# Stick-breaking attention on one core: scores and value products of four heads each in one run of matmuls

## The chip, the cores and the metric

The kernel runs on one core of a Trainium2 chip. The metric is the device time of one execution in microseconds (us), as the median of several runs. The engines are named as in the profile: PE is TensorE's matmul, PEld its weight load, DVE VectorE, ACT ScalarE, POOL GpSimd, SP the engine that issues most DMAs.

## The reference

A trunk of two layers on 256 tokens of 1024 features, in float32. Each layer has a mixer, cross attention into 256 memory tokens, and a squared-ReLU MLP. The mixer of the second (odd) layer is stick-breaking attention with 16 heads of 64 features:

```python
def _odd_mixer(h, w_in, w_out):
    s = h.shape[1]
    pos = jnp.arange(s)
    q, k, v = jnp.split(h @ w_in, 3, axis=-1)
    ...
        strict = pos[None, :] < t[:, None]
        z = jnp.einsum('bhqd,bhkd->bhqk', qb, k).astype(jnp.float32) * SB_SCALE
        log_beta = jax.nn.log_sigmoid(z)
        log_keep = jnp.where(strict, jax.nn.log_sigmoid(-z), 0.0)
        between = lax.cumsum(log_keep, axis=3, reverse=True) - log_keep
        a = jnp.where(strict, jnp.exp(log_beta + between), 0.0)
        return jnp.einsum('bhqk,bhkd->bhqd', a.astype(v.dtype), v)
    ...
    return _merge(o) @ w_out
```

So a key's weight is the sigmoid of its score times the product of sigmoid(-z) over all later keys that the query may see.

## The kernel before

The residual stream stays on chip, transposed: features on partitions, 256 tokens on the free axis. The weights stream through SBUF once, as units of [128, 1024] float32 (512 KB). SP loads a unit into one of four `raw` buffers; ACT casts it in two halves of 512 columns to a rounded part (`wh`, line 144), and DVE subtracts to get the remainder (`wl`, line 145); four units of each can stand ready. A projection takes three passes (high by high, high by low, low by high), so one unit is 24 matmuls of 256 columns (line 154). In the odd mixer the projections of a group's queries and keys are two units each; the values, with tokens on partitions, take two units that are both read by each token tile.

`mixer1` (lines 517 to 571) goes over four groups of four heads. For a group it projects q, k and v, and multiplies the queries and keys by the reciprocal norms on DVE (lines 528 and 531); ACT copies the values out of PSUM with theirs (`evac_nat`, line 253). Then it takes the group's heads in two pairs, `pp`. A head of a pair, `hh`, lies on 64 of the 128 partitions, so its score matmul uses 64 rows of the array (line 540):

```python
                for tt, (a, b, s) in enumerate(((0, 128, 128), (128, 384, 256))):
                    for hh in range(2):
                        rs = slice(64 * hh, 64 * hh + 64)
                        nc.tensor.matmul(ps[hh][:, a:b], lhsT=q[rs, pp, tt * P:(tt + 1) * P],
                                         rhs=k[rs, pp, 0:s], start=True, stop=True)
```

A head's scores are 384 columns: 128 keys for the first 128 queries, 256 keys for the second. These products are float32, and each is two records in the trace, one for each of two passes. For each head DVE adds the mask to the two diagonal blocks (548), ACT takes Sigmoid of -z (`keep`, 550) and of z (`beta`, 551), DVE scans `keep` backwards (552) and multiplies `beta` by the shifted scan in two pieces (555), and POOL sets the last column of each piece to zero (557). PE then transposes three blocks a head (`transposes`, line 309), ACT copies them out (311), and the value products follow (564), which write 64 partitions each, so they use 64 columns of the array. A pair's output is split into a rounded part and a remainder (165, 166).

After the fourth group come three parts of the cross attention's keys and values (`fill(1, 3)`) and the output projection. PE executes strictly in the order of the program, and that order is made by a scheduler from the program's dependencies and its own estimates: it moves the attention's matmuls of one group among the projections of the next, unless `keep_in_program_order` ties an instruction to the one that stands before it in the source.

PSUM has eight banks of 512 float32 columns: three `mm` for projections, two `sc`, and one each `tr`, `po`, `sm`. The scores use `sc`, the transposes `tr`, the value products `po`; `sm` is used for norms.

Of the kernel before, what the change touches and what calls it, by code (L numbers as in the profile page):

```python
"""Two-layer hybrid encoder trunk on one core.

The residual stream stays on chip, transposed: features on partitions, the 256 tokens on the free
axis.  Weights stream through SBUF once, in pieces of [128, 1024].  A float32 product of a weight
and an activation is taken as three float32r passes over an exact split of each operand into a
rounded part and its remainder (hi*hi + hi*lo + lo*hi).  The reciprocal norms of an RMSNorm are
applied to the products' results; its gains are applied to the activations before.
"""
# [9 lines left out]
F32 = mybir.dt.float32  # L18
F32R = mybir.dt.float32r
AF = mybir.ActivationFunctionType  # L20
# [3 lines left out]
P = 128  # L24
# [8 lines left out]
# columns of the constant table  # L33
# [6 lines left out]
C_END = 2688  # L40

# columns of the gain table
# [5 lines left out]
class Split:  # L48
    """Two float32r tiles, [128, 8, 256], that sum to a float32 activation."""
# [6 lines left out]
class Norm(Split):  # L56
    """An RMSNorm of a transposed stream whose reciprocal norm is applied later."""
# [6 lines left out]
    def part(self, src, kt):  # L64
        """Take feature tile kt, [128, 256], of the stream."""
# [25 lines left out]
class Builder:  # L91
# [26 lines left out]
    def ps(self, tag):  # L118
        """One bank of PSUM, from the banks of one kind of use."""
        return self.psum.tile([P, 512], F32, name="ps_" + tag, tag=tag, bufs=self.banks[tag])  # L120
# [4 lines left out]
    def unit(self, name, i, width=1024):  # L125
        """Load weight piece i of an array and split it into a rounded part and its remainder."""
        return self.unit_split(self.unit_load(name, i, width), 2)
# [21 lines left out]
    def passes(self, out, pairs, start=True, stop=True, pin=False, **kw):  # L149
        """out += sum of lhsT * rhs over float32 operands given as (hi, lo) pairs."""  # L150
# [12 lines left out]
    def split_into(self, hi, lo, src):  # L163
        """Exact split of src (SBUF or PSUM) into two float32r parts."""
        self.nc.scalar.copy(out=hi, in_=src)
        self.nc.vector.tensor_tensor(out=lo, in0=src, in1=hi.bitcast(F32), op=ALU.subtract)  # L166
# [6 lines left out]
    def rsqrt_split(self, acc, nat=True, out=None):  # L173
        """rsqrt_mean of one [128, 256] sum over D features, its sum taken in two float32r passes."""
# [10 lines left out]
    def rsqrt_mean(self, accs, n, w=T, nat=True, out=None):  # L185
        """1/sqrt(mean over partitions and tiles + eps) of summed squares, [128, w] on all
        partitions; with nat, columns 256, 257 hold it for both token tiles, tokens on partitions."""
# [6 lines left out]
    def rsqrt_of(self, ps, n, w=T, nat=False, out=None):  # L194
# [13 lines left out]
        # one Newton step: y * (1.5 - 0.5 * ms * y * y)  # L208
# [16 lines left out]
    def proj_t(self, units, n, ps, i):  # L225
        """n-tile i of ps (transposed result) from one [8 kt, 128] weight piece."""
# [10 lines left out]
    def proj_nat(self, name, i, n):  # L237
        """[tokens, 256 columns] for both token tiles, from two [4 kt, 256] pieces."""
# [17 lines left out]
    def out_proj(self, name, o, nxt):  # L256
        """Output projection into the residual stream; feeds the next norm tile by tile."""
# [25 lines left out]
    def fill(self, l, count):  # L283
        """Do up to count of the eight parts of layer l's keys and values."""
# [16 lines left out]
    def transposes(self, p2):  # L301
        """Probabilities of two heads, [t, (tile 0 | tile 1)], to [s, ...] with s on partitions:
        columns 0:256 keys 0..127 for all queries, 256:384 keys 128..255 for queries 128..255."""
# [15 lines left out]
    def softmax_rows(self, ps, tabs, scale, normalise):  # L319
        """exp(scale * (scores + table) - max) of two score tiles, each [t, 128 | 256]."""  # L320
# [27 lines left out]
    def scores(self, parts):  # L348
        """One head's causal scores, [t, 128 | 256]; parts: (q, k) with features on partitions."""
# [9 lines left out]
    def rope(self, dst, x, w):  # L359
        """x*cos + swap(x)*sin over w groups of 256 tokens; dst(rows) gives the place of 64 rows."""  # L360
# [12 lines left out]
    def mixer0(self, n, nxt, first):  # L373
        nc = self.nc
        # latent projections
# [40 lines left out]
        # keys and values of the latent attention  # L416
# [18 lines left out]
        # queries of the latent attention  # L435
# [83 lines left out]
    def mixer1(self, n, nxt):  # L519
# [3 lines left out]
        for g in range(4):  # L523
# [11 lines left out]
            for pp in range(2):  # L535
                ps = [self.ps("sc") for _ in range(2)]
                for tt, (a, b, s) in enumerate(((0, 128, 128), (128, 384, 256))):
                    for hh in range(2):
                        rs = slice(64 * hh, 64 * hh + 64)
                        nc.tensor.matmul(ps[hh][:, a:b], lhsT=q[rs, pp, tt * P:(tt + 1) * P],  # L540
                                         rhs=k[rs, pp, 0:s], start=True, stop=True)
                beta = self.k4.tile([P, 2, 384], F32, name="beta", tag="k4")
                keep = self.k4.tile([P, 2, 384], F32, name="keep", tag="k4")
                sfx = self.k4.tile([P, 2, 384], F32, name="sfx", tag="k4")
                for hh in range(2):
                    z, bt, kp, c = ps[hh][:, 0:384], beta[:, hh, :], keep[:, hh, :], sfx[:, hh, :]
                    diag = z.rearrange("p (b c) -> p b c", b=3)[:, 0::2, :]
# [444 lines left out]
```

## Time and profile before

| | |
|---|---|
| median of 3 runs | 830.42 us (830.34 to 831.72) |
| the profiled execution, first to last instruction | 829.1 us |
| PE busy | 814.9 us, 98% |
| DVE busy | 578.3 us, 70% |
| ACT busy | 448.8 us, 54% |
| mean granted clock of TensorE | 0.992 |
| DMA, mean over the span | 167 GB/s |

The span is that of the profiled execution; its whole time is not given beside it, and the runs' median is 1.3 us above its span, which is what lies around the first and the last instruction. A row of the timeline gives the start and the busy time of an instruction, or of several alike that follow each other (x8). Busy times of neighbours overlap, as PE and DVE are pipelined: what an instruction costs its engine is the step from its start to the next one's.

### The profile page before, as it was taken

The numbers are of one execution on the slowest core, as the hardware profiler recorded it, in microseconds if no ns is written. First come the engines' busy times: TensorE is split into PE (matmuls) and PEld (weight loads), VectorE is DVE, ScalarE is ACT, GpSimd is POOL, SyncE is SP. The second block draws the span as 40 slices with busy tenths as digits, with TensorE's granted clock in tenths as the row PEclk, the third lists the DMA queues.
The fourth block names the chain that finished last, engine by engine and source line by source line (L and its number), as shares of the span: only waits on it lengthen the run. The fifth ranks groups of instructions, "written<-read, shape, count | busy, mean of one in ns | idle before, by whom it ended". The sixth has DMA issues, their size and how long they took to land. (4 is left out here: it accounts for less than half of the span.)

```text
span 829.1 us, 15928 instructions
## 1 busy us (share of the span) xinstructions
PE 814.9 (98%) x6304; PEld 777.9 (94%) x6304; DVE 578.3 (70%) x1066; ACT 448.8 (54%) x924; POOL 60.8 (7%) x100
## 2 busy tenths in 40 slices
PE   8999999999999999999999999999999999999996
PEld 6989999999999999999988888899999999999995
DVE  7799865878686665566678565767759756666565
ACT  5667655756564444444466454565647544444443
POOL 6003000200020000000030000011003000000002
PEclk8999999999999999999999999999999999999998
DMA  8646245753356555555534433355436555555541
GB/s 306 208 133 204 92 162 182 225 181 107 122 186 204 196 180 178 184 186 190 180 129 153 151 120 112 130 175 167 144 97 208 183 195 183 177 187 192 179 152 51
DMA packets 38955, 138.62 MB, mean 167 GB/s; under 512 B 4449, under 2 KB 4705, under 8 KB 38753
## 3 DMA queue, kind: packets, MB, share of 16 engines
q1 hardware_dynamic: 38736, 137.35, 50.2%
q8 instruction: 49, 0.80, 0.4%
q10 hardware_dynamic: 144, 0.26, 0.1%
q14 instruction: 26, 0.20, 0.1%
HBM read 136.55 MB, written 1.05 MB: 166 GB/s over the span
## 5 line engine op out<-in xcount | busy, mean ns | idle before, releaser
L144 ACT CAST wh<-raw 128x512 fp32r<-128x512 f32 (+1 forms) x502 | 285.3, 618 | 273.3 <-issue 135.0
L145 DVE TENSOR_TENSOR wl<-raw,wh 128x512 fp32r<-128x512 f32 (+1 forms) x502 | 331.1, 699 | 142.4 <-ACT wh L144 141.4
L154 PE MATMUL ps_mm<-act_lo,wh 128*128 128x256 f32 x1248 | 356.8, 286 | 1.3 <-DVE act_lo L69 1.2
L154 PE MATMUL ps_mm<-act_hi,wl 128*128 128x256 f32 x1248 | 356.4, 286 | 1.5 <-DVE wl L145 1.5
L154 PE MATMUL ps_mm<-act_hi,wh 128*128 128x256 f32 x1248 | 354.3, 286 | 1.8 <-ACT wh L144 1.1
L154 PEld LDWEIGHTS ps_mm<-act_hi,wl 128*128 128x128 f32 x1248 | 240.2, 192 | 5.2 <-issue 3.0
L154 PEld LDWEIGHTS ps_mm<-act_hi,wh 128*128 128x128 f32 x1248 | 239.3, 192 | 5.2 <-issue 2.3
L154 PEld LDWEIGHTS ps_mm<-act_lo,wh 128*128 128x128 f32 x1248 | 240.0, 192 | 3.9 <-DVE act_lo L69 1.9
L83 POOL TENSOR_TENSOR sq<-sq 128x256 f32<-128x256 f32 x42 | 38.1, 908 | 480.7 <-ACT sq L79 479.6
L154 PE MATMUL ps_mm<-wh,act_hi 128*128 128x256 f32 x224 | 64.9, 290 | 0.0
L154 PE MATMUL ps_mm<-wl,act_hi 128*128 128x256 f32 x224 | 64.2, 287 | 0.6 <-DVE wl L145 0.6
L154 PE MATMUL ps_mm<-wh,act_lo 128*128 128x256 f32 x224 | 63.9, 285 | 0.0
L154 PEld LDWEIGHTS ps_mm<-wh,act_hi 128*128 128x128 f32 x224 | 42.8, 191 | 2.1 <-issue 1.7
L154 PEld LDWEIGHTS ps_mm<-wl,act_hi 128*128 128x128 f32 x224 | 42.8, 191 | 1.3 <-DVE wl L145 0.8
L154 PEld LDWEIGHTS ps_mm<-wh,act_lo 128*128 128x128 f32 x224 | 42.8, 191 | 1.2 <-issue 1.2
L628 DVE SCALAR_TENSOR_TENSOR m<-ps_mm,r 128x512 f32<-128x512 f32 x32 | 22.1, 690 | 27.8 <-PE ps_mm L154 27.8
L154 PE MATMUL ps_sc<-fl,wh 128*128 128x256 f32 x128 | 36.1, 283 | 0.0
L154 PE MATMUL ps_sc<-fh,wl 128*128 128x256 f32 x128 | 36.1, 283 | 0.0
L154 PE MATMUL ps_sc<-fh,wh 128*128 128x256 f32 x128 | 35.9, 283 | 0.0
L69 DVE SCALAR_TENSOR_TENSOR act_lo<-hT,gains,act_hi 128x256 fp32r<-128x256 f32 x48 | 32.4, 695 | 2.6 <-ACT act_hi L68 2.6
L68 ACT ACTIVATE act_hi<-hT,gains 128x256 fp32r<-128x256 f32 x48 | 23.6, 504 | 10.9 <-DVE hT L263 6.3
L154 PE MATMUL ps_sc<-wh,fh 128*128 128x512 f32 x64 | 25.3, 395 | 0.0
(229 smaller groups left out, 1136.8 us busy)
## 6 DMA issues: line engine op xcount, KB each, us to landing
raw<-in_w SPq DMA_DIRECT2D x128, 512.0 KB, 3.4
raw<-in_w_in SPq DMA_DIRECT2D x38, 512.0 KB, 3.4
raw<-in_xkv SPq DMA_DIRECT2D x32, 512.0 KB, 3.5
raw<-in_w_out SPq DMA_DIRECT2D x16, 512.0 KB, 3.3
raw<-in_wq SPq DMA_DIRECT2D x16, 512.0 KB, 3.9
raw<-in_wo SPq DMA_DIRECT2D x16, 512.0 KB, 3.3
raw<-in_memT SPq DMA_DIRECT2D x4, 512.0 KB, 3.8
cst<-in_cst SPq DMA_DIRECT2D x1, 1152.0 KB, 9.2
```

The source lines that it names most:

```text
L68: nc.scalar.activation(out=self.hi[:, kt, :], in_=src, func=AF.Copy, scale=g)
L69: nc.vector.scalar_tensor_tensor(out=self.lo[:, kt, :], in0=src, scalar=g, in1=self.hi[:, kt, :].bitcast(F32), op0=ALU.mult, op1=ALU.subtract)
L83: nc.gpsimd.tensor_tensor(out=self.acc, in0=self.acc, in1=sq, op=ALU.add)
L144: nc.scalar.copy(out=wh[:, s], in_=raw[:, s])
L145: nc.vector.tensor_tensor(out=wl[:, s], in0=raw[:, s], in1=wh[:, s].bitcast(F32), op=ALU.subtract)
L154: ins = self.nc.tensor.matmul(*args, **kws)
L628: nc.vector.scalar_tensor_tensor(out=m, in0=ps, scalar=0.0, in1=self.bc2(r), op0=ALU.max, op1=ALU.mult)
```

## The change

The work of the four heads of a group is gathered in a new function, `stick`. Its eight score matmuls are written one after the other, and all but the first are tied to the one before it (`pinned`). They go to four banks: for each head of a pair, `main` (an `sc` bank, all 512 columns: the first pair's second query tile in 0:256, the second pair's first tile in 256:384, the first pair's first tile in 384:512) and `rest` (`tr` or `sm`, the second pair's second tile). The elementwise operations then take 512 or 256 columns instead of 384, and the product with the scan is one piece. The transposes alternate between the banks `tr` and `sm`. The eight value products are written in one run as well and write the whole `po` bank, and the output is split in one piece of 512 columns. The constant table gets 128 more columns, a scan row of 512 instead of 384. In the last group, the first key and value parts behind the mixer are tied to stand after the scores (`issue_after`).

```diff
-C_END = 2688
+C_END = 2816
...
+    def pinned(self, *args, **kw):
+        self.tc.keep_in_program_order(self.nc.tensor.matmul(*args, **kw))
+
+    def stick(self, g, q, k, v, o):
...
+        main = [self.ps("sc") for _ in range(2)]
+        rest = [self.ps("tr"), self.ps("sm")]
+        first = True
+        for pp, tt, ps, a in ((1, 1, rest, 0), (0, 1, main, 0), (1, 0, main, 256), (0, 0, main, 384)):
+            for hh in (1, 0):
+                rs = slice(64 * hh, 64 * hh + 64)
+                w = P * (tt + 1)
+                (nc.tensor.matmul if first else self.pinned)(
+                    ps[hh][:, a:a + w], lhsT=q[rs, pp, tt * P:(tt + 1) * P], rhs=k[rs, pp, 0:w],
+                    start=True, stop=True)
+                first = False
+        scored = self.tc.nc.cur_bb.bb.instructions[-1]
+        probs = []
+        for ps, w, nd, pool, tag in ((main, 512, 3, self.k4, "k4"), (rest, 256, 1, self.k2, "k2")):
...
+            for hh in range(2):
+                z = ps[hh][:, 0:w]
+                diag = z[:, P:w].rearrange("p (b c) -> p b c", b=nd)
+                nc.vector.tensor_tensor(out=diag, in0=diag, op=ALU.add,
+                                        in1=self.sb_mask[:, None, :].broadcast_to([P, nd, P]))
+                nc.scalar.activation(out=keep[:, hh, :], in_=z, func=AF.Sigmoid, scale=-0.125)
+                nc.scalar.activation(out=beta[:, hh, :], in_=z, func=AF.Sigmoid, scale=0.125)
+                last = beta[:, hh, P:w].rearrange("p (b c) -> p b c", b=nd)[:, :, P - 1:P]
+                nc.gpsimd.memset(last, 0.0)
+                z, c = beta[:, hh, :], sfx[:, hh, :]
+                nc.vector.tensor_tensor_scan(out=c[:, ::-1], data0=keep[:, hh, ::-1],
+                                             data1=self.scan1[:, (512 - w):], initial=1.0,
+                                             op0=ALU.mult, op1=ALU.add)
+                nc.vector.tensor_tensor(out=z[:, 0:w - 1], in0=z[:, 0:w - 1], in1=c[:, 1:w],
+                                        op=ALU.mult)
+            probs.append(beta)
...
+        for pp in range(2):
+            t = self.k4.tile([P, 2, 384], F32, name="pT", tag="k4")
+            pT.append(t)
+            for hh in range(2):
+                ps = self.ps(("tr", "sm")[hh])
+                for b, (src, a) in enumerate(places[pp]):
+                    nc.tensor.transpose(out=ps[:, b * P:(b + 1) * P], in_=src[:, hh, a:a + P],
+                                        identity=self.ident)
+                nc.scalar.copy(out=t[:, hh, :], in_=ps[:, 0:384])
+        po = self.ps2("po")
+        first = True
+        for pp in (1, 0):
+            for blk, (a, b, t0) in enumerate(((0, 256, 0), (256, 384, 128))):
+                for hh in range(2):
+                    rs = slice(64 * hh, 64 * hh + 64)
+                    cs = slice((2 * pp + hh) * 64, (2 * pp + hh) * 64 + 64)
+                    (nc.tensor.matmul if first else self.pinned)(
+                        po[rs, pp, t0:T], lhsT=v[:, blk, cs], rhs=pT[pp][:, hh, a:b],
+                        start=blk == 0, stop=blk == 1)
+                    first = False
+        self.split_into(o.hi[:, 2 * g:2 * g + 2, :], o.lo[:, 2 * g:2 * g + 2, :], po)
+        return scored
...
     def mixer1(self, n, nxt):
...
-            for pp in range(2):
...
-                kt = 2 * g + pp
-                self.split_into(o.hi[:, kt, :], o.lo[:, kt, :], po)
+            scored = self.stick(g, q, k, v, o)
         self.tc.keep_in_program_order(
             nc.scalar.preload_act_table_set("natural_log_exp_and_others"))
-        self.fill(1, 3)
+        with self.tc.issue_after(scored):
+            self.fill(1, 3)
...
-        self.sb_mask, self.scan1 = col(C_SB, P), col(C_SCAN, 384)
+        self.sb_mask = col(C_SB, P)
+        self.scan1 = col(C_SCAN, 512)
...
-    last = np.zeros(384, np.float32)
-    last[[127, 383]] = 1.0
-    c[:, C_SCAN:C_SCAN + 384] = last[::-1]
+    last = np.zeros(512, np.float32)
+    last[[255, 383, 511]] = 1.0
+    c[:, C_SCAN:C_SCAN + 512] = last[::-1]
```

Where the instructions stand. A row gives the line, the operation, what is written and read, the tile's shape, and how many like it follow each other; `ps_mm<-act_hi,wh` is a projection matmul. PE before, group 1's scores, which stand among the query projections of group 2:

```order
L154 MATMUL ps_mm<-wh,act_lo 128x256
L540 MATMUL ps_sc<-sq_k,sq_q 128x128 x2
L540 MATMUL ps_sc<-sq_k,sq_q 128x256 x2
L154 MATMUL ps_mm<-act_hi,wh 128x256
...
L540 MATMUL ps_sc<-sq_k,sq_q 128x128
L540 MATMUL ps_sc<-sq_k,sq_q 128x256
L154 MATMUL ps_mm<-act_hi,wh 128x256
L154 MATMUL ps_mm<-act_lo,wh 128x256
L540 MATMUL ps_sc<-sq_k,sq_q 128x128
L540 MATMUL ps_sc<-sq_k,sq_q 128x256
L154 MATMUL ps_mm<-act_hi,wl 128x256
```

The first pair stands in one run; between it and the second pair's first head are 33 projection matmuls, and between that pair's heads two. In group 0 transposes stand between the two products of the last head as well. PE now, the same place:

```order
L154 MATMUL ps_mm<-wh,act_lo 128x256
L536 MATMUL ps_sm<-sq_k,sq_q 128x256
L520 MATMUL ps_tr<-sq_k,sq_q 128x256
L520 MATMUL ps_sc<-sq_k,sq_q 128x256 x2
L520 MATMUL ps_sc<-sq_k,sq_q 128x128 x4
L154 MATMUL ps_mm<-act_hi,wh 128x256
...
L571 MATMUL ps_sm<-cst,beta 128x128 x3
L154 MATMUL ps_mm<-act_hi,wl 128x256
...
L571 MATMUL ps_tr<-cst,beta 128x128 x3
```

All eight score matmuls stand together in every group, and 59 projection matmuls later come the first transposes. The value products, which before stood as one and three for each pair, are eight in a row in groups 1 to 3; in group 0 the first is alone, four projection matmuls ahead of the other seven. DVE now, behind group 1's scores:

```order
L549 TENSOR_TENSOR ps_sm<-ps_sm,cst 128x128
L549 TENSOR_TENSOR ps_tr<-ps_tr,cst 128x128
L145 TENSOR_TENSOR wl<-raw,wh 128x512 x2
L556 SCALAR_TENSOR_TENSOR sfx<-keep,cst 128x256
L549 TENSOR_TENSOR ps_sc<-ps_sc,cst 128x384
L556 SCALAR_TENSOR_TENSOR sfx<-keep,cst 128x256
L549 TENSOR_TENSOR ps_sc<-ps_sc,cst 128x384
L559 TENSOR_TENSOR beta<-beta,sfx 128x255 x2
L556 SCALAR_TENSOR_TENSOR sfx<-keep,cst 128x512 x2
L559 TENSOR_TENSOR beta<-beta,sfx 128x511 x2
L145 TENSOR_TENSOR wl<-raw,wh 128x512 x2
```

Before, two heads' operations stood between two weight splits; now those of all four heads do (the scan is printed as SCALAR_TENSOR_TENSOR). In group 0 a weight split stands behind each of the first two adds, and the query product of the next group ahead of the two wide products.

## Rows read from the trace of the kernel before

**Rows 1.** The page, part 1: busy time, share of the span and instructions of each engine.
```profile
PE 814.9 (98%) x6304; PEld 777.9 (94%) x6304; DVE 578.3 (70%) x1066; ACT 448.8 (54%) x924; POOL 60.8 (7%) x100
```

**Rows 2.** Busy times by stretches of the odd mixer (number of instructions), granted clock, DMA share, GB/s.
```profile
441.50:466.90 25.40, 25.40 (x190) 21.66 (x188) 16.63 (x33) 14.58 (x29) 0.54 (x8) 1.00 0.38 125
```

**Rows 3.** Who waited for whom, 441 to 545 us: us in total, times, longest.
```profile
DVE wl L145 <- ACT wh L144: 19.0, 10, 4.2
...
PEld ps_mm L154 <- issue: 7.7, 24, 0.4
```

**Rows 4.** PE's timeline, group 0, first score run: start, us, engine, line, what.
```profile
442.29 0.28 PE L154 MATMUL ps_mm<-act_lo,wh 128*128 128x256 f32 x1
442.50 0.93 PE L540 MATMUL ps_sc<-sq_k,sq_q 64*128 64x128 f32 x8
443.35 0.38 PE L154 MATMUL ps_mm<-act_hi,wl 128*128 128x256 f32 x1
443.58 0.28 PE L154 MATMUL ps_mm<-act_hi,wh 128*128 128x256 f32 x1
```

**Rows 5.** PE's timeline, group 1: one head of the second pair.
```profile
471.68 0.28 PE L154 MATMUL ps_mm<-act_lo,wh 128*128 128x256 f32 x1
471.80 0.28 PE L154 MATMUL ps_mm<-act_hi,wl 128*128 128x256 f32 x1
472.01 0.92 PE L540 MATMUL ps_sc<-sq_k,sq_q 64*128 64x128 f32 x4
...
473.08 0.28 PE L154 MATMUL ps_mm<-act_lo,wh 128*128 128x256 f32 x1
```

**Rows 6.** PE's timeline, group 0: the other head of the second pair, split by transposes.
```profile
448.53 0.49 PE L540 MATMUL ps_sc<-sq_k,sq_q 64*128 64x128 f32 x2
448.94 0.44 PE L309 MATMUL ps_tr<-cst,beta 128*128 128x128 f32 x2
449.31 0.70 PE L540 MATMUL ps_sc<-sq_k,sq_q 64*128 64x256 f32 x2
449.94 0.39 PE L154 MATMUL ps_mm<-act_lo,wh 128*128 128x256 f32 x1
```

**Rows 7.** PE's timeline, group 0: transposes and the first value product of a pair.
```profile
452.54 0.49 PE L309 MATMUL ps_tr<-cst,beta 128*128 128x128 f32 x3
452.96 0.65 PE L564 MATMUL ps_po<-pT,sq_v 128*64 128x256 f32 x2
...
453.76 0.28 PE L154 MATMUL ps_mm<-act_hi,wl 128*128 128x256 f32 x1
```

**Rows 8.** PE's timeline, group 0: the other three value products of its second pair.
```profile
463.91 0.28 PE L154 MATMUL ps_mm<-wl,act_hi 128*128 128x256 f32 x1
464.12 0.86 PE L564 MATMUL ps_po<-pT,sq_v 128*64 128x256 f32 x6
...
465.13 0.28 PE L154 MATMUL ps_mm<-wh,act_hi 128*128 128x256 f32 x1
```

**Rows 9.** DVE's timeline, group 1, behind its first score run.
```profile
467.97 0.76 DVE L548 TENSOR_TENSOR ps_sc<-ps_sc,cst 128x256 f32<-128x256 f32 x2 [0.29 <-PE ps_sc L540]
468.64 1.28 DVE L145 TENSOR_TENSOR wl<-raw,wh 128x512 fp32r<-128x512 f32 x2
469.84 1.80 DVE L552 TENSOR_TENSOR_SCAN sfx<-keep,cst 128x384 f32<-128x384 f32 x2
471.56 1.13 DVE L555 TENSOR_TENSOR beta<-beta,sfx 128x127 f32<-128x127 f32 x4
```

**Rows 10.** PE's timeline, group 1: its first score run.
```profile
467.01 0.93 PE L540 MATMUL ps_sc<-sq_k,sq_q 64*128 64x128 f32 x8
```

**Rows 11.** ACT's timeline: the table load of group 0, and two casts of group 1.
```profile
443.56 1.28 ACT L550 ACT_TABLE_LOAD   x1
...
467.85 1.14 ACT L144 CAST wh<-raw 128x512 fp32r<-128x512 f32 x2
```

**Rows 12.** The page, part 6: DMA issues, KB each, median us to landing.
```profile
cst<-in_cst SPq DMA_DIRECT2D x1, 1152.0 KB, 9.2
```

More of the change, by code (lines that the diff above doesn't have):

```diff
@@ L516, in mixer0 @@
         self.out_proj("w_out0", o_all, nxt)
+    def pinned(self, *args, **kw):
+        self.tc.keep_in_program_order(self.nc.tensor.matmul(*args, **kw))
+    def stick(self, g, q, k, v, o):
+        nc = self.nc
+        main = [self.ps("sc") for _ in range(2)]
[12 more added lines that the diff above has]
+        for ps, w, nd, pool, tag in ((main, 512, 3, self.k4, "k4"), (rest, 256, 1, self.k2, "k2")):
+            beta = pool.tile([P, 2, w], F32, name="beta", tag=tag)
+            keep = pool.tile([P, 2, w], F32, name="keep", tag=tag)
+            sfx = pool.tile([P, 2, w], F32, name="sfx", tag=tag)
+            for hh in range(2):
[14 more added lines that the diff above has]
+            probs.append(beta)
+        main, rest = probs
+        places = (((main, 384), (main, 0), (main, 128)), ((main, 256), (rest, 0), (rest, 128)))
+        pT = []
+        for pp in range(2):
[20 more added lines that the diff above has]
+        return scored
@@ L534, in mixer1 @@
             self.evac_nat(v, ps, r)
-            for pp in range(2):
[L536 to L547, printed above, removed]
-                    nc.vector.tensor_tensor(out=diag, in0=diag, op=ALU.add,
-                                            in1=self.sb_mask[:, None, :].broadcast_to([P, 2, P]))
-                    nc.scalar.activation(out=kp, in_=z, func=AF.Sigmoid, scale=-0.125)
-                    nc.scalar.activation(out=bt, in_=z, func=AF.Sigmoid, scale=0.125)
-                    nc.vector.tensor_tensor_scan(out=c[:, ::-1], data0=kp[:, ::-1], data1=self.scan1,
-                                                 initial=1.0, op0=ALU.mult, op1=ALU.add)
-                    for a, b in ((0, 127), (128, 383)):
-                        nc.vector.tensor_tensor(out=bt[:, a:b], in0=bt[:, a:b], in1=c[:, a + 1:b + 1],
-                                                op=ALU.mult)
-                        nc.gpsimd.memset(bt[:, b:b + 1], 0.0)
-                pT = self.transposes(beta)
-                po = self.ps("po")[:, 0:T]
-                for blk, (a, b, t0) in enumerate(((0, 256, 0), (256, 384, 128))):
-                    for hh in range(2):
-                        rs = slice(64 * hh, 64 * hh + 64)
-                        cs = slice((2 * pp + hh) * 64, (2 * pp + hh) * 64 + 64)
-                        nc.tensor.matmul(po[rs, t0:T], lhsT=v[:, blk, cs], rhs=pT[:, hh, a:b],
-                                         start=blk == 0, stop=blk == 1)
-                kt = 2 * g + pp
-                self.split_into(o.hi[:, kt, :], o.lo[:, kt, :], po)
```

## The prediction

> **What bounds the kernel now.** I read the busy shares first: TensorE (PE) is busy 98% of the span [rows 1]. Then the odd mixer's stage by stretches: in the one that begins with head group 0's scores, 25.4 us long, PE is busy for all of it at a granted clock of 1.00 (the 2.4 GHz level), while VectorE (DVE) works 16.6 us and ScalarE (ACT) 14.6 us [rows 2]. Then who waits for whom there: no PE wait of note for the attention's data stands in the view; what is large are the other engines' waits, for example DVE waiting 19.0 us for ACT's rounded weights. One row is unlike the rest: the weight load of the projections (PEld ps_mm) sat idle 7.7 us, 24 times, for nothing that the profile shows [rows 3]. Last, PE's timeline, which says what those 24 places are: each lies behind a run of score or value matmuls, which use half of the array (64 rows for scores, 64 columns for values). So this stage is as long as PE's instructions and the switches between whole and half array make it, and a change here is worth what it takes off PE, less what makes PE wait.
>
> **What a run costs now.** A projection matmul starts every 0.12 us (the first two starts) [rows 5]. In group 0's first score run, both heads of a pair, two 128-column and two 256-column products, each in two passes (8 records), lie between the starts 442.29 and 443.58 [rows 4]. That is 1.29 us, less the two projection pitches (0.24) it would have been: **1.05 us**. The second pair of a group is taken one head at a time. Such a run has 4 records, and lies between 471.80 and 473.08 [rows 5]: 1.28 - 0.24 = **1.04 us**. So half the work costs the same: the two heads of a pair run beside each other if they stand in one run, and each lone run pays for itself. How much of a run is columns? The split head of group 0 shows it: two 128-column passes reach the next start after 0.41 us, two 256-column passes after 0.63 [rows 6]. So 128 more columns are 0.11 us a pass, 256 are 0.22, the columns of one run 2 x 0.11 + 2 x 0.22 = 0.66, and the switch in and out is 1.05 - 0.66 = **0.39 us**.
>
> Values alike. The lone product (two 256-column passes) stands between 452.54 and 453.76 behind three transposes [rows 7]: 1.22 - 3 x 0.11 - 0.12 = **0.77 us**. The other three products of the pair, which overlap in part, stand between 463.91 and 465.13 [rows 8]: 1.22 - 0.24 = **0.98 us**, of which 0.66 are the columns of one head, so the switch is 0.32.
>
> **The change, part by part.** Scores before: 1.05 + 2 x 1.04 = 3.13 us a group, and group 0 one switch (0.39) more, where transposes split the last run [rows 6]: 4 x 3.13 + 0.39 = 12.9 us. Values before: two pairs of 0.77 + 0.98 a group: 4 x 3.50 = 14.0 us. Together **26.9 us**.
>
> After: eight score products stand in one run, head beside head. Its columns are those of two pairs, 2 x 0.66 = 1.32, with one switch 1.71; four groups 6.84. The value run: 1.32 + 0.32 = 1.64; four groups 6.56. In group 0 the order leaves one value product alone, four matmuls ahead of the other seven; the seven still fill the run, so that is one lone run more, 0.77. Together **14.2 us**. PE gives back 26.9 - 14.2 = **12.7 us**. Bounds: the switch was between 0.32 and 0.39 in all these runs, and eight runs by that difference are 0.6 us either way. A run this long is not in the trace; the sum assumes that the second pair's columns follow the first's at the pitch of rows 6.
>
> The number of transposes is the same (48), as are the copies behind them; each takes 0.11 us wherever it stands. The projections' order is the same but for what stands between them.
>
> Elementwise work. DVE's cost per operation is a small fixed part and the columns: two adds of 256 take 0.67 us, two weight splits of 512 1.20, two scans of 384 1.72 [rows 9]. So an add or product costs 0.07 + 0.00104 a column, a scan 0.07 + 0.0021 a column (an estimate from these rows): 384-column add 0.47, 128-column 0.20, scan of 512 1.12, of 256 0.60, product of 511 0.60, of 255 0.34. A group needs 2 x (0.47 + 1.12 + 0.60 + 0.20 + 0.60 + 0.34) = 6.7 us; before, 4 x (0.34 + 0.86 + 0.20 + 0.34) = 7.0. So hardly less: wider pieces save fixed parts only, and DVE's 16.6 us fit into a group of 22. I cost it at nothing on the path, as long as PE covers the **chain** from the scores to the first transposes. That cover is what the change alters, since the chain now runs through both pairs before any transpose.
>
> PE's side: from the first score to the next projection matmul 1.50 us, then 59 projection matmuls: the transposes are reached after 1.50 + 0.10 (the slow first step behind a switch) + 59 x 0.119 = **8.6 us**. DVE's side in groups 1 to 3: the weight split that stands between the adds and the scans waits for casts that ACT does behind the value copies; before, it started 1.63 us after the first score (468.64 against 467.01) [rows 9, 10]. Taking 1.5, as the add comes earlier: 1.5 + 1.2 (two splits) + 0.60 + 0.47 + 0.60 + 0.47 (small scans, wide adds) + 2 x 0.34 + 2 x 1.12 + 0.68 (first wide product) = **8.4 us**. So covered, by 0.2 us. In group 0, ACT must do two casts, from when the unit before is read (about 0.1 us after the first score), 1.1 us, and then load the Sigmoid table, 1.28 us, before the first keep [rows 11], which takes some 0.35; the first scan can start at 2.8, and DVE also has one query product (0.60) in the chain: 2.8 + 2 x 0.60 + 2 x (0.47 + 0.34) + 2 x 1.12 + 0.60 + 0.68 = **9.1 us**. So PE waits 0.5 us there, once. Ends of this term: 0 (if a cast or the load comes earlier) and 1 us in each group (rival 1).
>
> The Trainium skill, page "TensorEngine Tiling (Array Packing)", section "PSUM Bottleneck", speaks against a change of this kind: tiling speeds up TensorE but not the emptying of PSUM, which may become the bound. The trace agrees only in part: DVE's 16.6 us a group leave room in 22 us [rows 2], but the chain has 0.2 us to spare.
>
> Weights during the chain: DVE splits none for some 6 us. At its start four units stand split ahead (the pool's four), which are 4 x 24 x 0.12 = 11.5 us of PE. Covered. The constant table's DMA grows by 64 KB, from 1152 KB that land in 9.2 us [rows 12]; at that rate what stands behind it on SP's queue lands up to 0.5 us later, once, while PE works on weights already there: I take 0, with 0.5 as the end.
>
> **Sum.** -12.7 + 0.5 = -12.2 us. The profiled execution's span is 829.1 us; the runs' median, 830.42, is 1.3 us more, which lies around the span and stays. **818.2 us.**
>
> **Rivals.**
> 1. The elementwise chain comes late in every group. For it: 0.2 us to spare, and a scan of 512 not seen. Against: it was never late before [rows 3]. At 1 us of waiting in each of four groups in place of 0.5 in one: 818.2 + 3.5 = **821.7 us**.
> 2. The longer runs don't overlap two heads, and only the switches go. For it: value products of the same width have not been seen side by side in a run, only a wide beside a narrow [rows 8]. Against: the score pair in rows 4. Then a score run costs 2 x 1.32 + 0.39 = 3.03, a value run 2.96; 4 x 5.99 + 0.77 = 24.7 against 26.9: **828.7 us** with the wait, still faster.
> 3. Slower: the weights run dry. If the chain begins with fewer units split than counted, PE stops at the projection behind it. It decides from 12.7 / 4 = 3.2 us a group, that is, from two units missing (each 2.9 us of PE work): then 4 x 5.7 - 12.7 = +10: **840 us**. Against: the four units ahead, which PE's and DVE's orders show.
> 4. The change does less than it says, if the scheduler breaks the runs again: the order of PE shows them whole in groups 1 to 3, so this is worth the 0.77 already in the sum.
>
> **How the numbers follow.** Forecast 0.72, rival 1 0.18, rival 2 0.05, rival 3 0.03; 0.02 for what I don't see. The forecast's own width: 817.1 with no wait and cheap switches, 819.3 with the switches and the DMA at their other ends. The range goes on to rival 1, and 0.6 below for runs that stray: **816.5 to 822.0**. What a measurement of this kernel can tell from no change is about 0.2%, 1.7 us; every case but rival 3 and part of what I don't see lies beyond that on the fast side: faster 0.95, same 0.01, slower 0.04.
>
> **What would show it.** In the profile after: score runs of 16 records that take about 1.7 us from the last projection to the second next, less two pitches; value runs the same at 1.64; from one group's scores to the next some 22 us instead of 25; the idle time of the projections' weight load for "issue" at about nine places instead of 24. A PE wait for DVE's products before the transposes would be about 0.5 us in group 0 and under 0.2 in the others; if it is 1 us in all, rival 1. The prediction is wrong if group stretches shorten by less than 2.5 us, or if PE waits for weight splits in this stage.

## The result and the profile after

The changed kernel takes **818.95 us**, the median of 4 runs (818.56 to 819.69), beside 831.07 us of the kernel before on the same chip (830.34 to 832.17): a ratio of 0.9856, with a 95% interval of 0.9844 to 0.9868. It is 12.1 us faster; 818.2 was forecast. The profiled execution took 818.56 us, with a span of 816.4.

The page of the kernel after, its span and part 1:

```profile
span 816.4 us, 15863 instructions
...
PE 802.3 (98%) x6304; PEld 774.1 (95%) x6304; DVE 576.5 (71%) x1046; ACT 448.9 (55%) x920; POOL 60.6 (7%) x84
```

PE executes as many instructions as in [rows 1] and is busy 12.6 us less; DVE's and ACT's work is almost the same. The kernel after by stretches, each from the start of one group's scores to the next's (columns as in [rows 2]):

```profile
444.07:464.16 20.09, 19.85 (x164) 18.26 (x164) 14.76 (x25) 12.52 (x24) 0.41 (x4) 1.00 0.41 134
464.16:486.06 21.90, 21.90 (x189) 20.96 (x189) 15.45 (x27) 13.22 (x27) 0.40 (x4) 1.00 0.46 145
...
```

A full group takes 21.9 us, the third as the second; before, groups 2 and 3 began their scores 25.2 us apart. PE is still busy for all of it, at the same granted clock of 1.00 (the 2.4 GHz level), and DVE still has a quarter of the time free. Of these stretches only the first has idle time of PE, 0.24 us.

PE's timeline of the kernel after, group 1: its score run and its value run (records of one line and tile that follow each other are counted together under the first one's shape, so the x12 holds products of 256 and of 128 columns; records of the two heads start within 0.01 us of each other, as their products run side by side):

```profile
463.95 0.28 PE L154 MATMUL ps_mm<-wh,act_lo 128*128 128x256 f32 x1
464.16 0.48 PE L536 MATMUL ps_sm<-sq_k,sq_q 64*128 64x256 f32 x1
464.17 0.48 PE L520 MATMUL ps_tr<-sq_k,sq_q 64*128 64x256 f32 x1
464.48 0.38 PE L536 MATMUL ps_sm<-sq_k,sq_q 64*128 64x256 f32 x1
464.49 0.38 PE L520 MATMUL ps_tr<-sq_k,sq_q 64*128 64x256 f32 x1
464.70 1.04 PE L520 MATMUL ps_sc<-sq_k,sq_q 64*128 64x256 f32 x12
...
465.89 0.28 PE L154 MATMUL ps_mm<-act_lo,wh 128*128 128x256 f32 x1
...
480.01 0.28 PE L154 MATMUL ps_mm<-wh,act_hi 128*128 128x256 f32 x1
480.22 0.43 PE L581 MATMUL ps_po<-pT,sq_v 128*64 128x256 f32 x1
480.23 0.43 PE L520 MATMUL ps_po<-pT,sq_v 128*64 128x256 f32 x1
480.49 0.38 PE L581 MATMUL ps_po<-pT,sq_v 128*64 128x256 f32 x1
480.49 1.25 PE L520 MATMUL ps_po<-pT,sq_v 128*64 128x256 f32 x13
...
481.89 0.28 PE L154 MATMUL ps_mm<-wh,act_lo 128*128 128x256 f32 x1
```

By the prediction's measure, from the last projection's start before a run to the second one's behind it, less two pitches, the score run costs 465.89 - 463.95 - 0.24 = 1.70 us where [rows 4, 5] gave 1.05 + 2 x 1.04; the value run 481.89 - 480.01 - 0.24 = 1.64 where [rows 7, 8] gave 2 x (0.77 + 0.98).

Who waited for whom in the kernel after, 441 to 535 us (us in total, times, longest):

```profile
DVE wl L145 <- ACT wh L144: 14.7, 11, 4.0
...
PEld ps_mm L154 <- issue: 1.1, 5, 0.4
...
PEld ps_tr L571 <- DVE beta L559: 0.4, 1, 0.4
...
PE ps_tr L571 <- DVE beta L559: 0.2, 1, 0.2
```

The unexplained idle time of the projections' weight load, 7.7 us at 24 places in [rows 3], is down to 1.1 at five (about nine were forecast). New is one wait of PE for DVE, and the timeline gives its place in group 0:

```profile
452.62 0.28 PE L154 MATMUL ps_mm<-act_hi,wl 128*128 128x256 f32 x1
453.14 0.55 PE L571 MATMUL ps_tr<-cst,beta 128*128 128x128 f32 x3 [0.24 <-DVE beta L559]
```

From the last projection's start to the transposes are 0.52 us instead of 0.12: PE loses **0.40 us**.

**The stage.** Most of what follows is told by the odd mixer's stage: the time between two fixed matmuls on PE, one shortly ahead of group 0's scores (2.8 us in the changed kernel, 0.8 before) and one behind the last value products, with the same 800 matmuls outside the attention between them in every kernel. It was **127.83 us** before and is **115.65** after, 12.18 less. All later parts of the program are equal in the traces of the kernels before and after to some 0.01 us, and so is the time from 139 us to this stage; what is left are the first 139 us, whose matmuls are the same in all kernels. They differ from run to run (137.1 to 139.1 us over the traces of this case). So the stage shows tenths that the medians hide.

### The profile page after: what moved, and what is told of

Same layout as the page of the kernel before. It is cut to its first block, busy times and chain, and to the rows that moved or that the text cites. A ratio compares the mean times of both kernels' runs of the same rounds, so it can differ in the third digit from the quotient of the medians.

```text
span 816.4 us, 15863 instructions
## 1 busy us (share of the span) xinstructions
PE 802.3 (98%) x6304; PEld 774.1 (95%) x6304; DVE 576.5 (71%) x1046; ACT 448.9 (55%) x920; POOL 60.6 (7%) x84
## 3 DMA queue, kind: packets, MB, share of 16 engines
HBM read 136.61 MB, written 1.05 MB: 169 GB/s over the span
```

## Experiments

Each kernel's medians come from 4 or more runs, beside runs of the kernel before at 830.8 to 831.0 us. Diffs are against the changed kernel.

**The changed kernel once more.**

> The changed kernel itself, as the mark for the runs beside it. Both theories: 818.95 us within 0.7, and the same stage as before: score runs 1.70 us, value runs 1.64 us, one lone value product and one wait of 0.40 us before the first transposes in group 0.

819.63 us (819.46 to 820.19), ratio 0.9863 [0.985, 0.9877]; stage 115.65 again. The gain repeats, and so does the stage, to the last digit shown.

**The Sigmoid table loaded early.**

```diff
                 r = n.finish()
+                self.tc.keep_in_program_order(nc.scalar.preload_act_table_set("sigmoid_and_others"))
```

> The Sigmoid table is loaded right behind the reciprocal norms of the mixer, some 7 us before the first scores, in place of between the first scores and the first Sigmoid. My theory: the table load is what made PE wait 0.40 us in group 0, and with the chain earlier the scheduler also puts that group's eight value products in one run, which takes off a lone product of 0.77 us. So 1.2 us faster than the run beside it (817.8 if that is 818.95), with no wait of PE before group 0's transposes. Rival: the casts of weights ahead of the Sigmoids make the chain late, not the table; then the wait stays near 0.4 and the gain is the 0.77 alone.

817.51 us (817.28 to 818.24), ratio 0.9838 [0.9825, 0.9852]; stage 114.46, 1.19 less. ACT's timeline of this kernel:

```profile
434.65 1.28 ACT L595 ACT_TABLE_LOAD   x1
435.94 1.14 ACT L144 CAST wh<-raw 128x512 fp32r<-128x512 f32 x2
439.42 1.15 ACT L144 CAST wh<-raw 128x512 fp32r<-128x512 f32 x2 [2.33 <-PE ps_mm L154]
```

The load now stands where ACT is otherwise idle for 2.33 us soon after, and PE's wait of 0.40 us is gone, though the transposes stand 54 projection matmuls behind the scores instead of 59. With it the scheduler puts group 0's eight value products in one run (1.644 us instead of 0.769 + 1.639, 0.76 less). Both terms together are 1.16 of the 1.19. So the wait goes with the place of the table load, and a load of a table off the critical engine had a price by way of the order. How much of the 0.40 is the load itself this run does not separate, as two things moved: DVE's first scan starts 1.78 us behind the first score instead of 2.73 (in the changed kernel DVE is idle for 0.31 us there, for the Sigmoid behind the load), and the next group's query product, 0.58 us of DVE, no longer stands ahead of the wide products.

**Head by head in the score run.** The eight products stay in one run, but one head's four come first, then the other's.

```diff
-        for pp, tt, ps, a in ((1, 1, rest, 0), (0, 1, main, 0), (1, 0, main, 256), (0, 0, main, 384)):
-            for hh in (1, 0):
+        for hh in (1, 0):
+            for pp, tt, ps, a in ((1, 1, rest, 0), (0, 1, main, 0), (1, 0, main, 256), (0, 0, main, 384)):
```

> The eight score products still stand in one run, but the four of one head come first and then the four of the other. Theory A (each half of the array takes its own products in order and waits for nobody): the heads still pass side by side, the run stays at 1.7 us, the time within 0.5 us of the changed kernel's. Theory B (products start in program order, side by side only with their neighbour): the second head's first product starts only when the first head's last has started, so the columns pass nearly one head after the other: 2 x 1.32 - 0.2 instead of 1.32, a run of some 2.8 us, 4 x 1.1 = 4.4 us slower.

823.28 us (822.67 to 823.65), ratio 0.9905 [0.9892, 0.9919]; stage 119.09, 3.44 more. PE's timeline of this kernel, group 1's score run:

```profile
466.04 0.28 PE L154 MATMUL ps_mm<-wh,act_lo 128*128 128x256 f32 x1
466.25 0.70 PE L536 MATMUL ps_sm<-sq_k,sq_q 64*128 64x256 f32 x2
466.78 0.70 PE L520 MATMUL ps_sc<-sq_k,sq_q 64*128 64x256 f32 x3
467.22 0.48 PE L520 MATMUL ps_tr<-sq_k,sq_q 64*128 64x256 f32 x1
467.32 0.39 PE L520 MATMUL ps_sc<-sq_k,sq_q 64*128 64x128 f32 x2
467.54 0.38 PE L520 MATMUL ps_tr<-sq_k,sq_q 64*128 64x256 f32 x1
467.55 1.25 PE L520 MATMUL ps_sc<-sq_k,sq_q 64*128 64x128 f32 x7
468.72 0.39 PE L154 MATMUL ps_mm<-act_hi,wh 128*128 128x256 f32 x1
468.95 0.28 PE L154 MATMUL ps_mm<-act_lo,wh 128*128 128x256 f32 x1
```

The run takes 2.67 us instead of 1.70, with the same products and one switch in and out. The second head's first product (into `tr`) starts at 467.22, 0.97 us after the first head's, where the alternating order has it 0.01 us after: a head that stands behind the other's four products waits for most of them, and only the last 0.33 us of starts overlap. So the overlap of two heads comes from their alternation, not from their being in one run. Four runs cost 4 x 0.97 = 3.87 more; PE's wait in group 0 does not occur here, which gives 0.40 back; 3.47 by that, 3.44 measured. The Trainium skill's page "TensorE: Matmul & The Clock Gate", Part 3, section "The mechanism", says that matmuls of different tiles of the array overlap and start and end strictly in program order. For the starts these rows don't agree, if the program keeps the order to which the ties hold it: three of the first head's records (the two from 467.32 on and the first of those from 467.55 on) start behind 467.22. So PE's order, called strict ahead of the prediction, shows here within each head's products and not between the two heads'. Why the second head starts there, and not later, no run shows.

**Value products pair by pair**, as before the change, everything else as after.

```diff
+            po = self.ps("po")[:, 0:T]
             for blk, (a, b, t0) in enumerate(((0, 256, 0), (256, 384, 128))):
...
-                    (nc.tensor.matmul if first else self.pinned)(
-                        po[rs, pp, t0:T], lhsT=v[:, blk, cs], rhs=pT[pp][:, hh, a:b],
-                        start=blk == 0, stop=blk == 1)
+                    nc.tensor.matmul(po[rs, t0:T], lhsT=v[:, blk, cs], rhs=t[:, hh, a:b],
+                                     start=blk == 0, stop=blk == 1)
```

> The change's scores, but the value products written pair by pair and untied, each pair in its own half of the bank, as before. With the transposes alternating between two banks the order then still has a pair's four products together in groups 1 to 3 (in group 0 one is alone). My theory: two runs of 0.66 + 0.33 in place of one of 1.64, so 0.34 us a group, 4 x 0.34 = 1.3 us slower than the changed kernel in this stage; so most of the 6.6 us that the value products gained comes from two heads standing side by side, not from eight in a run. Rival: the run of eight is what gains; then 5 to 6.6 us slower.

820.04 us (819.93 to 821.35), ratio 0.9878 [0.9863, 0.9893]; stage 116.77, 1.12 more. In groups 1 to 3 each pair's four products now stand in one run by themselves, without ties, and cost 0.95 and 0.99 us: 1.94 a group, against 3.47 before the change and 1.64 after. So of the 1.83 us that a group's values gained, 1.53 came from a pair's first product no longer standing alone and 0.30 from joining the pairs. That the transposes' two banks let the scheduler do the first is likely, but not shown by itself; they are not enough, for where the scores go pair by pair (below) a value product stands alone again with these same banks.

**A whole-array product in the middle of the score run.** A transpose with all 128 rows, into columns that are written again behind it, cuts the run in two (`n_run` counts the turns of the outer loop).

```diff
...
+            if n_run == 2:
+                self.tc.keep_in_program_order(nc.tensor.transpose(
+                    out=main[1][:, 256:384], in_=q[:, 0, 0:P], identity=self.ident))
```

> One transposition of a block of queries, whose result is overwritten at once, stands in the middle of each score run, so that the array goes to the whole and back once more in each group. It is work beyond the reference's; the outputs stay the same. My theory: 0.11 us for the block and a switch of 0.39 us more in each group, 4 x 0.50 = 2.0 us slower than the changed kernel in this stage. Rival (a switch costs nothing by itself, only the heads' passing side by side counts): 4 x 0.11 = 0.4 us.

820.5 us (820.21 to 821.8), ratio 0.9884 [0.9867, 0.99]; stage 117.17, 1.52 more. PE's timeline of this kernel, group 1, the score run without its first products:

```profile
464.64 0.28 PE L154 MATMUL ps_mm<-wh,act_lo 128*128 128x256 f32 x1
...
465.38 0.60 PE L520 MATMUL ps_sc<-sq_k,sq_q 64*128 64x256 f32 x4
465.91 0.33 PE L535 MATMUL ps_sc<-cst,sq_q 128*128 128x128 f32 x1
466.17 0.71 PE L520 MATMUL ps_sc<-sq_k,sq_q 64*128 64x128 f32 x8
466.81 0.39 PE L154 MATMUL ps_mm<-act_hi,wh 128*128 128x256 f32 x1
467.04 0.28 PE L154 MATMUL ps_mm<-act_lo,wh 128*128 128x256 f32 x1
```

The run grows from 1.70 to 2.16 us, by 0.46: 0.11 for the block's own columns and **0.35 for one switch to the whole array and back**. Four of these are 1.84; group 0's wait falls from 0.40 to 0.06, which leaves 1.50 of the 1.52.

**Without ties.**

```diff
     def pinned(self, *args, **kw):
-        self.tc.keep_in_program_order(self.nc.tensor.matmul(*args, **kw))
+        self.nc.tensor.matmul(*args, **kw)
```

> The ties between the matmuls of a run are taken away; what is left of the change is that the four heads' work is written together. The order of PE then differs in group 0 alone: one score product stands three projection matmuls behind the other seven. My theory (the order on PE is all that counts): one lone product of 256 columns, 0.44 + 0.39 us, while the run of seven stays as long as before, since its partner's place is empty: 0.8 us more, minus up to 0.4 for a wait of group 0 that may be covered. 0.4 to 0.8 us slower than the changed kernel in this stage, so at most 0.1% in the time. Rival: the ties are what makes the gain; then most of 12 us is lost.

819.68 us (818.92 to 819.95), ratio 0.9869 [0.9854, 0.9883]; stage 116.02, 0.37 more. Only group 0's score run breaks: 14 records for 1.695 us and a lone product for 0.814, so 0.81 more, and PE's wait of 0.40 is gone: 0.41 by these, 0.37 measured. The other runs hold together unaided: the banks and the order in the source do the work, and the ties guard one place.

**Scores pair by pair**, with the 384-column elementwise operations of before; values as after.

```diff
-        main = [self.ps("sc") for _ in range(2)]
-        rest = [self.ps("tr"), self.ps("sm")]
...
+        for pp in range(2):
+            ps = [self.ps("sc") for _ in range(2)]
+            for tt, (a, b, s) in enumerate(((0, 128, 128), (128, 384, 256))):
...
```

> The change's value products, but the scores pair by pair, untied, with the narrow elementwise pieces of before. The order has three score runs in groups 0 to 2 as before, in group 3 one run with the second pair head by head; the first value product of each group stands alone. My theory: scores 3.1 to 3.5 us in groups 0 to 2 against 1.70, in group 3 some 1.3 more than 1.70 less two switches (heads one after the other, but in one run): 1.4 + 1.4 + 1.8 + 0.6 = 5.2; and a lone value product (0.77) in three groups more: 2.3. So 7.5 us slower than the changed kernel in this stage, that is 4.7 us faster than before. Rival: the wider elementwise pieces carry part of the gain; then it is slower still, by what DVE saves (some 0.3 us a group, 1 us in all), and PE waits for DVE.

828.9 us (827.77 to 831.83, 10 runs), ratio 0.998 [0.9968, 0.9993]; stage 126.18, 10.53 more, 3 us beyond the expectation. Most of the change's gain is lost. In groups 0 to 2 the scores are the three runs of before (1.05, 1.04, 1.04 us), and in every group a value product stands alone again (0.77 + 1.64, so 2.28 more in all). What was not foreseen is group 3. PE's timeline of this kernel:

```profile
513.57 0.93 PE L535 MATMUL ps_sc<-sq_k,sq_q 64*128 64x128 f32 x8
516.36 1.68 PE L535 MATMUL ps_sc<-sq_k,sq_q 64*128 64x128 f32 x8 [1.87 <-ACT beta L547]
517.97 0.41 PE L154 MATMUL ps_mm<-act_hi,wh 128*128 128x256 f32 x1
```

and its stretches there:

```profile
516.30:517.97 1.67, 1.61 (x9) 1.04 (x9) 1.67 (x3) 0.77 (x3) 0.27 (x4) 1.00 0.65 226
517.97:521.23 3.26, 3.26 (x18) 3.26 (x17) 2.90 (x8) 1.55 (x4) 0.13 (x2) 0.53 0.33 124
521.23:522.27 1.04, 1.04 (x9) 1.04 (x8) 1.00 (x3) 0.28 (x2) 0.13 (x2) 0.82 0.00 0
522.27:527.00 4.73, 4.73 (x43) 4.73 (x42) 2.58 (x6) 3.05 (x7) 0.00 (x0) 1.00 0.15 54
```

The scheduler put the second pair's scores right behind the first pair's. They need the two `sc` banks, which ACT's Sigmoids had not yet read, and PE stood idle for 1.87 us. The second score run lasts 1.61 us from its start to the projection behind it, where 0.85 is usual [rows 4]. That is not the clock, which is still 1.00 there: the heads stand one behind the other in this run, as was expected, and their records start 0.11 to 0.22 us apart as in a lone head's run. Behind it the granted clock is 0.53, near the 1.2 GHz level: projection matmuls start every 0.21 us instead of 0.12, and from 517.97 to 522.27 PE takes 4.30 us for what would take some 2.80 at the usual pitches (an estimate from the steps in this trace); from 522.27 on the clock is 1.00 again. The terms: scores 13.95 us over the four groups instead of 6.81, so +7.14 (the 1.87 and the 0.76 of heads one after the other are in it); values +2.28; the slow matmuls +1.5; group 0's wait, which is absent here, -0.4: **10.5 of the 10.53**. So four banks for the scores buy one run in place of three, and in the changed kernel no score waits for a Sigmoid. What the wider elementwise operations are worth by themselves no run shows.

**Each scan twice.** This asks how much cover the elementwise chain has left.

```diff
+                nc.vector.tensor_tensor_scan(out=c[:, ::-1], data0=keep[:, hh, ::-1],
+                                             data1=self.scan1[:, (512 - w):], initial=1.0,
+                                             op0=ALU.mult, op1=ALU.add)
```

> Each scan runs twice, which adds 2 x 1.12 + 2 x 0.60 = 3.4 us to DVE's work of a group. The scheduler, which knows of it, places the transposes 87 projection matmuls behind the scores instead of 59, and lets some other instructions stand between the score products or between the value products. Theory (the stage is as long as PE's instructions and switches, and the elementwise chain only has to end before the place where the transposes stand): the added DVE work itself is free, and the stage grows by what the broken runs cost, 0.4 for a switch and up to 0.7 for a pair's lone products in some groups, 1 to 3 us in all. Rival (the elementwise work has become the bound): the added 3.4 us in each of four groups come through, +13 us or a little less.

827.14 us (826.49 to 827.8), ratio 0.9953 [0.9939, 0.9966]; stage 122.16, **6.51 more**: between both expectations, and neither is right. Who waited for whom in this kernel, 440 to 550 us:

```profile
PE ps_sm L574 <- DVE beta L562: 3.2, 4, 1.5
...
PE ps_tr L574 <- ACT pT L576: 1.7, 1, 1.7
```

In group 0 the transposes stand 87 projection matmuls behind the scores instead of 59, 3.3 us later, which ought to cover nearly all of the added 3.4 us; yet the wait there grows from 0.40 to 1.64. DVE's timeline of this kernel, the end of group 0's chain, shows why:

```profile
456.46 0.67 DVE L145 TENSOR_TENSOR wl<-raw,wh 128x512 fp32r<-128x512 f32 x1
457.04 1.22 DVE L559 TENSOR_TENSOR_SCAN sfx<-keep,cst 128x512 f32<-128x512 f32 x1
458.18 0.66 DVE L145 TENSOR_TENSOR wl<-raw,wh 128x512 fp32r<-128x512 f32 x1
```

Two weight splits of 0.58 us each now stand among the scans, so the chain grew from 9.0 to 13.6 us, by 4.6 and not 3.4. In group 1 five splits and a query product stand in it, where the changed kernel has two splits. In all PE waits for DVE at four places and once for the copies: five transposes start 0.67 to 1.95 us behind the matmul ahead of them, 5.7 us beyond the usual pitch in all. The attention's runs cost 1.0 more, as first score products stand alone, and the transposes behind a wait 0.2; less the 0.4 that group 0 waited before there are some 6.4 of the 6.5. So the elementwise chain is a near neighbour of PE as the bound of the stage, and what lengthened it was in part the order: other DVE work that the scheduler put into it.

**Values right ahead of the next scores**, with the early table load: the value run of a group is issued as the first thing of the next group's score run, and the scores are tied to it.

```diff
-        first = True
+        first = values is None
+        if values is not None:
+            values()
         for pp, tt, ps, a in ((1, 1, rest, 0), (0, 1, main, 0), (1, 0, main, 256), (0, 0, main, 384)):
...
```

> As the run before (table early), and each group's value products stand directly ahead of the next group's scores, so that 64-column products are followed by 64-row ones with no whole-array matmul between. Theory A (the switch is paid at each way in and out of the whole array): three of the four boundaries lose one way out and one way in; the two runs apart cost 0.39 + 0.33 us of switching, one fused run some 0.4 to 0.5, so 0.2 to 0.3 us each, 0.6 to 1.0 us faster in all than the run with the early table. Theory B (any change of the array's division costs the same, halves by row to halves by column too): no gain, within 0.2 us.

818.12 us (817.74 to 818.26), ratio 0.9843 [0.9829, 0.9856]; but the stage is 113.95, 0.51 less than with the early load alone. The first 139 us were 138.55 in this trace and 137.14 in the other, which hid it. So both ran again, side by side:

> The kernel with the early table load once more, with the next one beside it. If the time ahead of the odd mixer (the program's first 139 us, which are the same instructions in all these kernels) varies from run to run and not from kernel to kernel, the total comes out anywhere from 817.3 to 819 us, while the odd mixer's stage is again 114.5 us.

> The value run directly ahead of the next group's scores, once more. The odd mixer's stage is again 0.5 us shorter than with the early table load alone (113.95). If the first 139 us vary only from run to run, the median is 0 to 1 us below that of the kernel beside it; if they belong to the kernel, it is again some 0.6 us above, at about 818.1.

The early load gave 818.27 us (817.65 to 818.34, ratio 0.9844 [0.9831, 0.9858]), the values ahead of the scores **817.61** (816.93 to 817.77, ratio 0.9837 [0.9823, 0.985]); the stages repeat as 114.46 and 113.95, and the first 139 us are 138.27 and 138.28 this time. So that part varies from run to run. By the stage the last kernel is the fastest of the study, by 0.5 us; by the medians of both rounds (818.12 and 817.61 against 817.51 and 818.27) it can't be told from the early load. PE's timeline of it, at the joint:

```profile
462.52 1.25 PE L520 MATMUL ps_po<-pT,sq_v 128*64 128x256 f32 x13
463.70 0.48 PE L520 MATMUL ps_sm<-sq_k,sq_q 64*128 64x256 f32 x1
```

Between the projections around it (462.04 and 465.43, less the 0.24) a joint run costs 3.15 us where the two apart cost 1.64 + 1.70 = 3.35: 0.19 less. Three times that is 0.58, and the stage shows 0.51. With 2 x 1.32 for the columns as in the prediction, 0.51 of the joint run is switching, against 0.71 of the two apart and some 0.35 of one: a step from 64 columns to 64 rows of the array costs less than the way by the whole array, but more than nothing.

## Why the prediction was right

- **What bounds the stage.** PE's instructions and switches did, and do: stretches are 3.3 us shorter at the same busy share and clock.
- **The runs before**, 26.9 us: 12.88 for scores and 13.89 for values, 26.8 together in the trace.
- **The runs after**, 14.2: four score runs of 1.70 (1.71 said), three value runs of 1.64 (1.64), and 0.77 + 1.64 in group 0: 14.15. PE gave back 12.6 (12.7). The switch, taken as 0.39 and 0.32 from the split head and the pair's end, is 0.35 by the cut run.
- **The chain in group 0**, 9.1 us against 8.6, so a wait of 0.5: it took 9.0, and the wait was 0.40. The early load took the wait away, with the order that came with it.
- **The chain in groups 1 to 3**, 8.4 us, covered by 0.2. DVE's timeline of the kernel after, group 1, the chain's last operations, and then PE's, the transposes that wait for them:

```profile
469.62 2.33 DVE L556 TENSOR_TENSOR_SCAN sfx<-keep,cst 128x512 f32<-128x512 f32 x2
471.87 1.26 DVE L559 TENSOR_TENSOR beta<-beta,sfx 128x511 f32<-128x511 f32 x2
473.05 0.68 DVE L145 TENSOR_TENSOR wl<-raw,wh 128x512 fp32r<-128x512 f32 x1
```

```profile
472.83 0.49 PE L571 MATMUL ps_sm<-cst,beta 128*128 128x128 f32 x3
```

  A scan of 512 columns costs half of 471.87 - 469.62, 1.13 us (1.12 estimated), a product half of 473.05 - 471.87, 0.59 (0.60). The first product ends at 472.53, so the chain took 8.4 us from 464.16, as estimated, and the transposes start 0.3 us behind it. In group 0, where PE does wait, they start 0.06 behind it, so 0.2 were to spare, as was forecast.
- **Rival 1** (late in every group) has fallen for this kernel, but the doubled scans show what lay behind it: 3.4 us more of scans a group cost 6.5 in the stage.
- **Rival 2** (no overlap in long runs) has fallen: equal wide products run side by side. Head by head the same products cost 2.67, near the 3.03 that it gave, so the source's alternation decides.
- **Rival 3** (weights run dry): no wait of PE for a split in the stage, and DVE's wait for ACT's rounded weights fell from 19.0 to 14.7 us. **Rival 4**: only group 0's lone value product, which was in the sum.
- **PSUM.** Here too the measurement decides on the section of the Trainium skill that the prediction weighed ("TensorEngine Tiling (Array Packing)", "PSUM Bottleneck"): the emptying of PSUM became no bound in groups 1 to 3 of this kernel, with 0.2 us to spare; where the scores had two banks only, PE waited for it at one place, 1.87 us, as the order put one pair's scores right behind the other's. The section speaks of a fourfold speed-up of TensorE; here two heads share it.
- **The sum**, -12.2 in the stage, was -12.18. That it fits to 0.02 is luck: 12.7 was 12.6, and 0.5 was 0.40. The total of 818.95 instead of 818.2 has other terms. The profiled span came out at 816.4, not 816.9, as the first 139 us were 0.5 shorter in this run; the four runs' spans are 816.4 to 817.5. And the time around the span was the step that was off: the prediction took 1.3 us from a median and a span of different executions and let it stay. In executions whose own time is known it is 1.7 to 1.9 for the kernel before and 2.1 to 2.2 for the changed one, so it was 0.5 too small and it did not stay. It goes with the kernel (1.7 to 1.9 also with values by pair, scores by pair and doubled scans); the cause is open.

What stays open: which tenths of the switch belong to going in and which to coming out, and why the first 139 us vary; as they vary by 2 us, the larger constant table, put at 0 with 0.5 as its end, can't be seen in them. The tie of the first key and value parts in the last group was not tested by itself.

## What to carry to other kernels

Where PE bounds a stage and matmuls use half of its array, count the places where it changes between half and whole, and look whether the two halves' products alternate in the program: here a place cost 0.35 us, and alternating was worth 1 us in a run of 1.7. More banks for such a run let more products stand in it, and here kept them from waiting for the readers of a bank; then see by how much the now longer chain behind it is covered, for here it was 0.2 us. To see tenths, time a stage between two fixed instructions, as a start that varies by a microsecond hides them in the total.

## What the runs showed of the chip

- A pause of PE of 1.87 us was followed, 1.6 us after its end, by a granted clock of 0.53 for 3.26 us and of 0.82 for 1.04 us, which cost 1.5 us beside the pause itself; in the kernel with doubled scans pauses of 1.48 and 1.68 us were followed by none (the granted clock stayed 1.00). So a pause can cost nearly twice its length; these are one case each. Three of the ten executions with scores pair by pair took 830.5 to 831.8 us at a mean granted clock of 0.989, the other seven 827.8 to 829.0 at 0.992 to 0.996; what sets them apart no trace shows.
- Going from half the columns to half the rows of the array without the whole array between saved 0.19 of two switches of some 0.35.
- The table load took 1.28 us, and the first Sigmoid started 1.30 us after its start (445.09 and 446.39, in the changed kernel). The Trainium skill's page "ScalarE: Activation LUTs", section "What ACT_TABLE_LOAD costs", gives about 2.66 us a switch, with a drain beside the load; no such drain shows here, and the measurement decides.
